# Mixture-of-experts stage of a transformer block in f32: another order of the gate, up and down products, and the low parts of the weights on one engine

## The chip, the cores and the metric

One core of one Trainium2 chip runs the whole block. The metric is device time in microseconds (us) of one launch; a profile of one execution shows each engine (PE = TensorE, with PEld its weight loads; ACT = ScalarE; DVE = VectorE; POOL = GpSimd; SP = SyncE, which here only issues DMAs).

## What is computed

The block is attention plus pooling plus convolution, an output projection, and then an expert-choice feed-forward network and a last normalisation. The change touches only the expert part:

```
aff = softmax(h @ w_router)                     # 1024 rows, 16 experts
g, idx = top_k(aff.T, 128)                      # each expert takes 128 rows
xg = h[idx]                                     # 16 x 128 x 2048
y = (silu(xg @ w_gate) * (xg @ w_up)) @ w_down * g
x = x + mod[5] * scatter_add(idx, y);  out = rmsnorm(x, final_g)
```

Per expert `w_gate` and `w_up` are 2048 x 1024 and `w_down` is 1024 x 2048, all f32: 24 MiB of weights an expert, read once from device memory, 384 MiB in all.

## The kernel before, in words

**Split products.** A product in f32 is made of three products in the fp32r format: high x high, high x low and low x high. A weight's high part is a cast on ACT (line 1393), its low part is the weight minus the high part (line 1397), on DVE, and for every third half unit on POOL. The activations are split in the same way after a transpose on PE (`transpose_split`, lines 1457 to 1465).

**Units.** The weights come in 24 units of 1 MiB an expert (`units`, from line 1349): a unit is two k-tiles of 128 rows by 1024 columns, so two half units. `fetch` (line 1371) loads a unit into one of 11 buffers (8 in the pool `er`, 3 in `er1`) through SP's queue; `half_unit` splits half a unit into one of 6 buffers `es_t`, asks for the load of the unit 11 places on, and hands the parts to 6 matmuls of 512 columns (3 products, 2 column halves), all through the helper at line 176. An expert thus has 48 half units and 288 such matmuls.

**Order within an expert** (from line 1504). The units of gate and up alternate, both results growing in two PSUM tiles `gu`. Then come Silu on ACT (line 1526), the product with up on DVE (line 1527), four groups of transposes for the next expert's rows (`turn_rows`: `xh`, `xl`, one buffer each) and the gather of the rows of the expert after that, two groups of transposes for this expert's hidden rows (`hh`, `hl`), and then down, as two halves of 8 half units, through one PSUM tile `dn`. DVE scales each half into `y` (line 1555), and a POOL-queue DMA adds `y` into the rows of `acc` (line 1559). A row of multipliers `M5` is built by `on_rows` ahead of the first expert: POOL makes diagonal tiles, PE multiplies them by ones.

**The last expert** also carries the eight final tiles (`final_tile`: load from `acc`, normalise, store), placed by the list `fin` at eighths of the gate-up part and quarters of the down halves; they use `er` buffers and SP's queue.

**Queues.** Every engine works its own queue in order. The order of a queue is not quite the written one: a list scheduler with a simulated timeline places the instructions, so next-expert matmuls can stand between those of the last down steps.

Of the kernel before, what the change touches and what calls it, by code (L numbers as in the profile page):

```python
# [9 lines left out]
F32 = mybir.dt.float32  # L10
F32R = mybir.dt.float32r
# [3 lines left out]
AF = mybir.ActivationFunctionType  # L15
ALU = mybir.AluOpType
# [4 lines left out]
P = 128  # L21
D = 2048
KT = D // P
# [5 lines left out]
NQB = SEQ // QB  # L29
HEADS = 8  # L30
NE = 16
CAP = 128
FF = 1024
NFT = FF // P
# [16 lines left out]
    first=58,  # L51
# [31 lines left out]
    er=8,  # L83
    e0=[3, 7, 11],
    eh=4,
    fin=[2, 4, 6, 8, 10, 11, 12, 13],
    wdve=0,
    z_val=3,
    z_n1=1,
# [41 lines left out]
def raw(ap):  # L131
    return ap.bitcast(F32)
# [36 lines left out]
def block_kernel(tc, I, out, dbg=None):  # L169
    nc = tc.nc  # L170
    pe, act, dve, gp, sp = nc.tensor, nc.scalar, nc.vector, nc.gpsimd, nc.sync
# [3 lines left out]
    def mm(o, l, r, start=True, stop=True):  # L175
        return pe.matmul(o, l, r, start=start, stop=stop, skip_group_check=True)  # L176
# [12 lines left out]
    acc = dr.tile([SEQ, D], F32, name="acc")  # L189
# [35 lines left out]
    fg_col = colB[:, 49:65]  # L225
# [1120 lines left out]
        ln2(i)  # L1346
    mk.close("lnx")
    er0 = mk("er0", bufs=3, side="right")
    units = []
    for e in range(NE):  # L1350
        for k in range(KT // 2):
            units.append((e, "g", k))
            units.append((e, "u", k))
        for half in range(2):
            for k in range(4):
                units.append((e, "d", (half, k)))

    def unit_src(u):
        e, kind, k = u
# [28 lines left out]
    def split(i, kk, early=None):  # L1388
        if i < len(units) and (i, kk) not in splits:
            fetch(i)  # L1390
            r = raws[i][:, kk]
            s = es_.tile([P, 2, 1024], F32R, name="es_t", tag="es")
            c = act.copy(s[:, 0], r)  # L1393
            if early:
                nosync(tc, c, last_exp[0])
            on_gp = 2 * i + kk < 4 if early else (2 * i + kk) % 3 == 2
            lo = (gp if on_gp else dve).tensor_tensor(s[:, 1], r, raw(s[:, 0]), op=ALU.subtract)  # L1397
            if early and not on_gp:
                nosync(tc, lo, early)
            splits[i, kk] = s  # L1400

    def half_unit(i, kk):
        split(i, kk)
        if kk == 0:
            fetch(i + PRE)
        else:
            raws.pop(i)
        return splits.pop((i, kk))
# [42 lines left out]
    def gather(e):  # L1451
        xg = ex.tile([P, D], F32, name="xg", tag="xg", bufs=1)
        ins = gp.indirect_dma_start(out=xg, out_offset=None, in_=h2S,
                                    in_offset=bass.IndirectOffsetOnAxis(ap=idxT[:, e:e + 1], axis=0))
        return xg, ins

    def transpose_split(x, n, hi, lo):
        for g in range(n // 4):
            t = pet.tile([P, 512], F32, name="tre", tag="tr")
            for q in range(4):  # L1460
                k = 4 * g + q
                pe.transpose(t[:, q * P:(q + 1) * P], x[:, k * P:(k + 1) * P], ident)  # L1462
            tv = t.rearrange("p (k n) -> p k n", n=P)
            act.copy(hi[:, 4 * g:4 * g + 4], tv)
            dve.tensor_tensor(lo[:, 4 * g:4 * g + 4], tv, raw(hi[:, 4 * g:4 * g + 4]), op=ALU.subtract)

    def final_rows(x, j):
        rms_stats(x, j, [ex.tile([P, D], BF16, name="dump_f", tag="xg", bufs=1)])
        dve.scalar_tensor_tensor(x, x, rst[:, j:j + 1], FG, op0=ALU.mult, op1=ALU.mult)

    def final_tile(i):
        xf = er.tile([P, D], F32, name="xf", tag="er")
        sp.dma_start(xf, acc[i * P:(i + 1) * P])
        final_rows(xf, i)
        sp.dma_start(out[i * P:(i + 1) * P], xf)

    ui = 0
    xg = [gather(0)]
    for i in range(PRE, PRE + 3):
        fetch(i, gp, xg[0][1])  # L1480

    def turn_rows(e):
        xh = ex.tile([P, KT, P], F32R, name="xh", tag="xh", bufs=1)
        xl = ex.tile([P, KT, P], F32R, name="xl", tag="xl", bufs=1)
        transpose_split(xg.pop()[0], KT, xh, xl)
        if 0 < e + 1 < NE:
            xg.append(gather(e + 1))
        return xh, xl

    xnext = turn_rows(0)  # L1490
    ones = ex.tile([P, P], F32, name="ones")
    dve.memset(ones, 1.0)

    def on_rows(dst, col):
        for g in range(4):
            t = pet.tile([P, 512], F32, name="tre", tag="tr")
            for q in range(4):
                dg = ex.tile([P, P], F32, name="dg", tag="dg", bufs=2)
                gp.tensor_scalar(dg, ident, col[:, 4 * g + q:4 * g + q + 1], 1.0, op0=ALU.mult, op1=ALU.mult)  # L1499
                mm(t[:, q * P:(q + 1) * P], ones, dg)  # L1500
            act.copy(dst[:, g * 512:(g + 1) * 512], t)

    M5 = ex.tile([P, D], F32, name="M5")
    on_rows(M5, mods[:, 5])
    for e in range(NE):
        xh, xl = xnext
        gu = [pgu.tile([P, 1024], F32, name=f"gu{i}", tag=f"gu{i}") for i in range(2)]
        for k2 in range(KT // 2):
            if e == NE - 1:
                if k2 == 0:  # L1510
                    FG = er.tile([P, D], F32, name="FG", tag="er")
                    on_rows(FG, fg_col)
                for i in range(NQB * 2):
                    if T["fin"][i] == k2:
                        final_tile(i)
            for w in range(2):
                for kk in range(2):
                    k = 2 * k2 + kk
                    s = half_unit(ui, kk)
                    for lhs, wl, first, last in ((xh, 0, True, False), (xh, 1, False, False), (xl, 0, False, True)):  # L1520
                        for c in range(2):
                            mm(gu[w][:, c * 512:(c + 1) * 512], lhs[:, k, :], s[:, wl, c * 512:(c + 1) * 512],
                               start=(k == 0 and first), stop=(k == KT - 1 and last))
                ui += 1
        hs = ex.tile([P, FF], F32, name="hs", tag="hs", bufs=1)
        act.activation(hs, gu[0], AF.Silu)
        dve.tensor_tensor(hs, hs, gu[1], op=ALU.mult)
        if e + 1 < NE:
            xnext = turn_rows(e + 1)
        hh = ex.tile([P, NFT, P], F32R, name="hh", tag="hh", bufs=1)  # L1530
        hl = ex.tile([P, NFT, P], F32R, name="hl", tag="hl", bufs=1)
        transpose_split(hs, NFT, hh, hl)
        y = ex.tile([P, D], F32, name="y", tag="y", bufs=1)
        last = e == NE - 1
        if last:
            xr = er.tile([P, D], F32, name="xr", tag="er")
            gp.indirect_dma_start(out=xr, out_offset=None, in_=acc,
                                  in_offset=bass.IndirectOffsetOnAxis(ap=idxT[:, e:e + 1], axis=0))
        for half in range(2):
            dn = pdn.tile([P, 1024], F32, name="dn", tag="dn")  # L1540
            for k2 in range(4):
                if last:
                    for i in range(NQB * 2):
                        if T["fin"][i] == 8 + 4 * half + k2:
                            final_tile(i)
                for kk in range(2):
                    k = 2 * k2 + kk
                    s = half_unit(ui, kk)
                    for lhs, wl, first, fin in ((hh, 0, True, False), (hh, 1, False, False), (hl, 0, False, True)):
                        for c in range(2):  # L1550
                            mm(dn[:, c * 512:(c + 1) * 512], lhs[:, k, :], s[:, wl, c * 512:(c + 1) * 512],
                               start=(k == 0 and first), stop=(k == NFT - 1 and fin))
                ui += 1
            hsl = slice(half * 1024, (half + 1) * 1024)
            dve.scalar_tensor_tensor(y[:, hsl], dn, gT[:, e:e + 1], M5[:, hsl], op0=ALU.mult, op1=ALU.mult)  # L1555
            if last:
                dve.tensor_tensor(y[:, hsl], y[:, hsl], xr[:, hsl], op=ALU.add)
        if not last:
            gp.indirect_dma_start(out=acc, out_offset=bass.IndirectOffsetOnAxis(ap=idxT[:, e:e + 1], axis=0),
                                  in_=y, in_offset=None, compute_op=ALU.add)  # L1560
        else:
            final_rows(y, 8)
            gp.indirect_dma_start(out=out, out_offset=bass.IndirectOffsetOnAxis(ap=idxT[:, e:e + 1], axis=0),
                                  in_=y, in_offset=None)

    if "h2" in dbg:
        sp.dma_start(dbg["h2"], h2S)
# [30 lines left out]
```

## Time and profile before

| | before |
|---|---|
| median of 3 runs | 3542.62 us (3541.07 to 3546.62) |
| the profiled execution, own time | 3547.89 us |
| its span | 3546.1 us |
| mean granted TensorE clock | 0.937 |
| first and last matmul of the expert stage | 2185.2 and 3516.8 us |
| busy over the span | PE 88%, DVE 70%, ACT 52%, POOL 47% |

The span is read by stretches: the expert stage is its last 1361 us, and an expert's period is the time from the second half of one down product to that of the next. "Idle before" in a row is the time in which the engine stood still ahead of those instructions, with what ended it. "DMA share" is the mean busy share of the 16 DMA engines in a stretch; records of packets overlap a little, so it can read just over 1. A clock of 1.00 is the upper of TensorE's two levels, 0.50 the lower.

### The profile page before, as it was taken

What the parts mean: (1) busy time and instruction counts of PE and PEld (TensorE: products, weight loads), DVE (VectorE), ACT (ScalarE), POOL (GpSimd) and SP (SyncE); (2) the same over time, 40 slices, a digit from 0 to 9 for tenths busy, and PEclk for the clock granted to TensorE, in tenths of its full rate; (3) what the DMA queues carried; (4) which work ended last, traced back from release to release, by engine and by line L of the source; (5) the groups of instructions that cost most, each with busy time, mean ns of one, the idle gap of its engine ahead of it and who ended that gap; (6) DMA issues with size and microseconds to landing.
All of it is one profiled execution on the core that took longest, in us unless ns stands there. A gap on an engine that the chain in (4) does not pass through costs nothing.

```text
span 3546.1 us, 48685 instructions
## 1 busy us (share of the span) xinstructions
PE 3130.5 (88%) x18527; PEld 2672.3 (75%) x18527; DVE 2496.6 (70%) x2523; ACT 1833.1 (52%) x2585; POOL 1673.7 (47%) x863
## 2 busy tenths in 40 slices
PE   7789999999897979788999795988889989999985
PEld 4678889888786868668899794777667767777774
DVE  5676766641356566765756687888888888888877
ACT  5433322451355545544554344666666666666665
POOL 1551100110554544535666776655555555665664
PEclk9899999999998989889999997999999999999997
DMA  9667787632654544555878777999999898999987
GB/s 309 185 210 244 276 282 263 198 107 79 198 168 129 159 146 142 178 171 180 278 232 279 246 257 265 320 326 341 330 331 329 315 333 325 333 334 326 343 303 283
DMA packets 489564, 891.23 MB, mean 251 GB/s; under 512 B 24913, under 2 KB 339874, under 8 KB 478450
## 3 DMA queue, kind: packets, MB, share of 16 engines
q1 hardware_dynamic: 465488, 791.42, 64.8%
q0 software_dynamic: 23744, 96.68, 9.1%
q8 instruction: 145, 2.38, 0.3%
q14 instruction: 89, 0.73, 0.1%
q10 hardware_dynamic: 98, 0.03, 0.0%
HBM read 797.80 MB, written 90.23 MB: 250 GB/s over the span
## 4 chain that ended last, share of the span: by engine, by line
PE 28%; DVE 12%; issue 10%; POOL 6%; DMA 3%; ACT 3%; POOLq 0%; SPq 0%; DVEq 0%; ACTq 0%
PE gu L176 10%; PE dn L176 8%; DVE es_t L1397 6%; PE gm L176 5%; POOL w_split L424 3%; PE sc L176 1%; POOL es_t L1397 1%; PE tre L1462 1%; PE av L176 1%; ACT es_t L1393 1%; DMA cv_z<-zS 1%; DMA w_raw<-in_w_out 1%; DVE nm L935 1%; DMA nbc<-sclS 1%; POOL dg L1499 1%
## 5 line engine op out<-in xcount | busy, mean ns | idle before, releaser
L1397 DVE TENSOR_TENSOR es_t<-er_t,es_t 128x1024 fp32r<-128x1024 f32 x509 | 1008.3, 2026 | 166.3 <-ACT es_t L1393 165.5
L1393 ACT CAST es_t<-er_t 128x1024 fp32r<-128x1024 f32 x768 | 797.2, 1050 | 343.1 <-PE gu L176 173.2
L1397 POOL TENSOR_TENSOR es_t<-er_t,es_t 128x1024 fp32r<-128x1024 f32 x259 | 719.8, 2781 | 456.4 <-ACT es_t L1393 456.2
L424 POOL TENSOR_TENSOR w_split<-w_raw,w_split 128x1024 fp32r<-128x1024 f32 x208 | 549.3, 2649 | 388.0 <-ACT w_split L423 367.1
L176 PE MATMUL g_x<-hxh,w_split 128*128 128x512 f32 (+3 forms) x2560 | 596.9, 344 | 18.7 <-DVE w_split L424 13.0
L176 PE MATMUL gu<-es_t,xh 128*128 128x512 f32 x2048 | 579.6, 400 | 11.9 <-DVE es_t L1397 10.9
L423 ACT CAST w_split<-w_raw 128x1024 fp32r<-128x1024 f32 x288 | 301.7, 1049 | 373.9 <-PE g_x L176 109.0
L176 PEld LDWEIGHTS gu<-es_t,xh 128*128 128x128 f32 x2048 | 378.8, 188 | 112.0 <-DVE es_t L1397 25.3
L176 PEld LDWEIGHTS g_x<-hxh,w_split 128*128 128x128 f32 x2560 | 402.6, 192 | 66.0 <-DVE w_split L424 14.6
L176 PE MATMUL gm<-w_split,mxh 128*128 128x256 f32 x2048 | 392.7, 290 | 9.1 <-POOL w_split L424 3.5
L176 PEld LDWEIGHTS gm<-w_split,mxh 128*128 128x128 f32 x2048 | 327.3, 195 | 16.6 <-DVE oy L1097 4.8
L176 PE MATMUL g_x<-hxl,w_split 128*128 128x256 f32 (+1 forms) x1280 | 337.1, 341 | 1.3 <-DVE hxl L396 1.3
L176 PE MATMUL dn<-es_t,hh 128*128 128x512 f32 x1024 | 307.7, 422 | 28.2 <-DVE y L1555 26.6
L176 PE MATMUL gu<-es_t,xl 128*128 128x512 f32 x1024 | 322.7, 396 | 0.0
L176 PE MATMUL gm<-w_split,mxl 128*128 128x256 f32 x1024 | 296.5, 290 | 1.1 <-DMA mxl<-mixP 1.1
L935 DVE TENSOR_REDUCE nm<-sc 128x1 f32<-128x1280 f32 x128 | 190.6, 1489 | 130.7 <-PE sc L176 85.5
L176 PE MATMUL gm<-hbh,w_split 128*128 128x256 f32 x1280 | 255.2, 294 | 21.3 <-ACT e_raw L497 14.6
L176 PEld LDWEIGHTS dn<-es_t,hh 128*128 128x128 f32 x1024 | 204.1, 203 | 86.0 <-ACT es_t L1393 29.8
L308 DVE SCALAR_TENSOR_TENSOR ada_a<-ada_w,st,ada_a 128x1024 f32<-128x1024 f32 x150 | 226.6, 1510 | 42.0 <-DMA ada_w<-in_w_ada 38.9
L176 PEld LDWEIGHTS gm<-hbh,w_split 128*128 128x128 f32 x1280 | 209.1, 197 | 28.8 <-ACT e_raw L497 18.2
L176 PEld LDWEIGHTS gu<-es_t,xl 128*128 128x128 f32 x1024 | 192.0, 188 | 45.8
L176 PEld LDWEIGHTS g_x<-hxl,w_split 128*128 128x128 f32 x1280 | 201.5, 191 | 24.9 <-DVE hxl L396 2.5
(300 smaller groups left out, 4887.5 us busy)
## 6 DMA issues: line engine op xcount, KB each, us to landing
er_t<-in_w_down SPq DMA_DIRECT2D x128, 1024.0 KB, 7.9
er_t<-in_w_gate SPq DMA_DIRECT2D x127, 1024.0 KB, 9.5
er_t<-in_w_up SPq DMA_DIRECT2D x126, 1024.0 KB, 6.6
ada_w<-in_w_ada SPq DMA_DIRECT2D x192, 512.0 KB, 5.5
w_raw<-in_w_in SPq DMA_DIRECT2D x160, 512.0 KB, 4.5
w_raw<-in_w_out SPq DMA_DIRECT2D x128, 512.0 KB, 5.0
ks<-kS POOLq DMA_DIRECT2D x16, 1280.0 KB, 8.3
vh<-vS POOLq DMA_DIRECT2D x16, 640.0 KB, 5.8
```

The source lines that it names most:

```text
L176: return pe.matmul(o, l, r, start=start, stop=stop, skip_group_check=True)
L308: dve.scalar_tensor_tensor(a, wt, col(k), a, op0=ALU.mult, op1=ALU.add)
L423: act.copy(s[:, 0], r)
L424: lo_eng.tensor_tensor(s[:, 1], r, raw(s[:, 0]), op=ALU.subtract)
L935: r = dve.tensor_reduce(nm, s, axis=AX, op=ALU.max, negate=True)
L1393: c = act.copy(s[:, 0], r)
L1397: lo = (gp if on_gp else dve).tensor_tensor(s[:, 1], r, raw(s[:, 0]), op=ALU.subtract)
L1462: pe.transpose(t[:, q * P:(q + 1) * P], x[:, k * P:(k + 1) * P], ident)
L1499: gp.tensor_scalar(dg, ident, col[:, 4 * g + q:4 * g + q + 1], 1.0, op0=ALU.mult, op1=ALU.mult)
```

## The change

- A list `plan` of stages takes the place of the loop body. The order is gate 0, up 0, then for experts 1 to 14: gate e, first half of down e-1, up e, second half of down e-1. At the end come both halves of down 14, then gate 15, up 15 and both halves of down 15. The units are fetched in that order; gate and up no longer alternate.
- Work beside the products is hung on steps (`beside`): the transposes of the rows of expert e (2 to 14) on steps 1, 3, 5, 7 of the second half of down e-2; those of the hidden rows of e (0 to 13) on steps 2 and 4 of gate e+1; `M5` on steps 6 to 12 of gate 1 instead of ahead of expert 0. Expert 1's rows are turned at the end of up 0, expert 14's hidden rows at the end of down 13, and expert 15's rows and hidden rows at the ends of down 14 and up 15.
- The down halves of experts 14 and 15 use `dn` and then a gate or up PSUM tile in turn.
- The final tiles are placed anew, over gate, up and down of expert 15.
- All low parts of weights, but for the four at the very start, are taken on DVE.

```diff
-    fin=[2, 4, 6, 8, 10, 11, 12, 13],
+    fin=[("g", 6), ("g", 12), ("u", 2), ("u", 8), ("u", 13), ("0", 2), ("0", 6), ("1", 2)],
...
+    plan = [("g", 0), ("u", 0)]
+    for e in range(1, NE - 1):
+        plan += [("g", e), ("d", e - 1, 0), ("u", e), ("d", e - 1, 1)]
+    plan += [("d", NE - 2, 0), ("d", NE - 2, 1), ("g", NE - 1), ("u", NE - 1), ("d", NE - 1, 0), ("d", NE - 1, 1)]
     units = []
-    for e in range(NE):
-        for k in range(KT // 2):
-            units.append((e, "g", k))
-            units.append((e, "u", k))
...
+    for kind, e, *half in plan:
+        units += [(e, kind, (half[0], k) if half else k) for k in range(4 if half else KT // 2)]
...
-            on_gp = 2 * i + kk < 4 if early else (2 * i + kk) % 3 == 2
+            on_gp = early and 2 * i + kk < 4
...
+    def turn_x(e, g):
+        if g == 0:
+            X_[e] = [ex.tile([P, KT, P], F32R, name=n, tag=n, bufs=1) for n in ("xh", "xl")]
+        turn_group(xg[e][0], g, *X_[e])
+        if g == 3:
+            xg.pop(e)
+            if e + 1 < NE:
+                xg[e + 1] = gather(e + 1)
...
+    for e in range(1, NE):
+        stage = ("u", 0) if e == 1 else ("d", e - 2, 1) if e < NE - 1 else ("d", NE - 2, 1)
+        for g in range(4):
+            add(stage, 15 if e == 1 else 2 * g + 1, turn_x, e, g)
     for e in range(NE):
...
+        for g in range(2):
+            if e < NE - 2:
+                add(("g", e + 1), 2 + 2 * g, turn_h, e, g)
+            elif e == NE - 2:
+                add(("d", e - 1, 1), 7, turn_h, e, g)
+            else:
+                add(("u", e), 15, turn_h, e, g)
+    for g in range(4):
+        add(("g", 1), 6 + 2 * g, on_rows, M5, mods[:, 5], [g])
+    for i, (kind, k) in enumerate(T["fin"]):
+        add((kind, NE - 1) if kind in "gu" else ("d", NE - 1, int(kind)), k, final_tile, i)
...
+    for stage in plan:
+        kind, e = stage[:2]
...
+        if kind == "d":
+            half = stage[2]
+            bank = pdn if half == 0 or e < NE - 2 else pgu
+            o = bank.tile([P, 1024], F32, name="dn", tag="dn" if bank is pdn else "gu" if e == NE - 2 else "gg")
...
+            o, lhss, nk = pgu.tile([P, 1024], F32, name="g" + kind, tag="g" + kind), X_[e], KT
+        for k in range(nk):
+            s = half_unit(ui, k % 2)
+            for lhs, wl, first, fin in ((lhss[0], 0, True, False), (lhss[0], 1, False, False), (lhss[1], 0, False, True)):
+                for c in range(2):
+                    mm(o[:, c * 512:(c + 1) * 512], lhs[:, k, :], s[:, wl, c * 512:(c + 1) * 512],
+                       start=(k == 0 and first), stop=(k == nk - 1 and fin))
...
+            for f, args in beside.get((stage, k), ()):
+                f(*args)
```

`turn_group` is one group of `transpose_split` as it was: four transposes, the cast on ACT, the subtraction on DVE.

## Rows read from the trace of the kernel before

**Rows 1.** The page, DMA busy tenths and GB/s in 40 equal slices:
```profile
DMA  9667787632654544555878777999999898999987
GB/s 309 185 210 244 276 282 263 198 107 79 198 168 129 159 146 142 178 171 180 278 232 279 246 257 265 320 326 341 330 331 329 315 333 325 333 334 326 343 303 283
```

**Rows 2.** Stretches of the expert stage: us, each engine's busy, PEclk, DMA share, GB/s:
```profile
2185.00:2261.29 76.29, 68.86 (x314) 55.28 (x313) 57.09 (x39) 50.86 (x56) 56.00 (x31) 0.94 0.84 299
2261.29:3334.13 1072.84, 967.88 (x4048) 761.64 (x4049) 925.14 (x534) 701.50 (x715) 616.68 (x235) 0.94 0.92 331
3334.13:3415.00 80.87, 74.36 (x313) 58.97 (x314) 68.07 (x40) 52.39 (x54) 45.09 (x18) 0.94 0.88 317
3415.00:3491.50 76.50, 64.62 (x285) 50.99 (x283) 62.84 (x38) 50.24 (x52) 60.21 (x31) 0.93 0.80 278
3491.50:3546.10 54.60, 23.36 (x92) 18.19 (x92) 34.00 (x25) 24.32 (x24) 17.67 (x13) 0.75 0.76 300
```

**Rows 3.** Timeline of one gap between up and down (2733 to 2744 us):
```profile
2733.91 0.63 PE L176 MATMUL gu<-es_t,xl 128*128 128x512 f32 x2
...
2739.17 1.94 PE L1462 MATMUL tre<-cst,xg 128*128 128x128 f32 x8 [4.63 <-DVE xl L1465]
...
2743.45 2.07 PE L176 MATMUL dn<-es_t,hh 128*128 128x512 f32 x4
```

**Rows 4.** Stretches of 3 us across a gap (columns as in rows 2):
```profile
2652.00:2655.00 3.00, 0.00 (x0) 0.00 (x0) 2.98 (x3) 2.04 (x4) 1.61 (x1) 0.99 1.02 359
2655.00:2658.00 3.00, 2.02 (x9) 1.65 (x10) 2.71 (x4) 1.17 (x2) 0.35 (x1) 0.50 0.87 314
```

**Rows 5.** Waits, thirteen periods from 2261 to 3334 us: us, times, longest:
```profile
PE dn L176 <- DVE y L1555: 21.6, 13, 1.9
```

**Rows 6.** The DMA queue's own waits over the same thirteen periods:
```profile
SPq L1371 <- DVE es_t L1397: 749.2, 313, 9.9
```

**Rows 7.** Short stretches (columns as in rows 2), two dips, then three full ones:
```profile
2664.00:2670.00 6.00, 6.00 (x27) 4.86 (x26) 4.30 (x3) 4.60 (x5) 4.21 (x2) 1.00 0.49 164
2748.00:2754.00 6.00, 6.00 (x27) 4.83 (x26) 3.44 (x3) 4.40 (x5) 3.79 (x2) 1.00 0.35 135
...
2619.00:2649.00 30.00, 28.63 (x121) 22.35 (x121) 29.48 (x14) 19.95 (x20) 18.34 (x7) 1.00 1.00 384
2703.00:2739.00 36.00, 30.21 (x128) 23.31 (x126) 35.09 (x18) 24.59 (x25) 21.25 (x8) 0.97 1.01 379
...
2622.00:2625.00 3.00, 3.00 (x15) 2.41 (x14) 2.48 (x3) 2.88 (x3) 1.75 (x1) 1.00 1.03 421
```

**Rows 8.** The chain that ended last: 39 matmuls in a row:
```profile
2273.19 9.12 PE gu L176 x39
```

**Rows 9.** DMA of the thirteen periods: bytes, two kinds of queue, median us to landing:
```profile
DMA packets 88661, 355.16 MB, mean 331 GB/s; under 512 B 5408, under 2 KB 5408, under 8 KB 85275
...
q0 software_dynamic: 3744, 27.26, 9.8%
...
acc<-y,idxT POOLq DMA_INDIRECT x13, 12.0
xg<-h2S,idxT POOLq DMA_INDIRECT x13, 9.1
```

**Rows 10.** Groups by line, thirteen periods: count, busy us, mean ns, idle before:
```profile
L1397 DVE TENSOR_TENSOR es_t<-er_t,es_t 128x1024 fp32r<-128x1024 f32 x417 | 833.8, 2047 | 127.5 <-ACT es_t L1393 126.9
L1397 POOL TENSOR_TENSOR es_t<-er_t,es_t 128x1024 fp32r<-128x1024 f32 x209 | 580.4, 2778 | 401.3 <-ACT es_t L1393 401.2
L1462 PE MATMUL tre<-cst,xg 128*128 128x128 f32 x200 | 41.6, 340 | 58.6 <-DVE xl L1465 58.6
```

**Rows 11.** Timeline of DVE, two low parts: beside a POOL subtraction, then alone:
```profile
2757.94 2.21 DVE L1397 TENSOR_TENSOR es_t<-er_t,es_t 128x1024 fp32r<-128x1024 f32 x1
2760.91 1.23 DVE L1397 TENSOR_TENSOR es_t<-er_t,es_t 128x1024 fp32r<-128x1024 f32 x1 [0.77 <-ACT es_t L1393]
```

**Rows 12.** Timeline of PE: transposes between gate and up matmuls of a running expert:
```profile
2690.17 0.49 PE L1462 MATMUL tre<-cst,xg 128*128 128x128 f32 x3
```

**Rows 13.** Timeline of the end: the last matmuls and the last store:
```profile
3516.54 0.62 PE L176 MATMUL dn<-es_t,hl 128*128 128x512 f32 x2
...
3538.24 1.03 POOL L1563 DMA_INDIRECT out<-y,idxT  x1 [4.16 <-DMA out<-xf]
```

More of the change, by code (lines that the diff above doesn't have):

```diff
@@ L1348, in block_kernel @@
     er0 = mk("er0", bufs=3, side="right")
+    plan = [("g", 0), ("u", 0)]
+    for e in range(1, NE - 1):
+        plan += [("g", e), ("d", e - 1, 0), ("u", e), ("d", e - 1, 1)]
+    plan += [("d", NE - 2, 0), ("d", NE - 2, 1), ("g", NE - 1), ("u", NE - 1), ("d", NE - 1, 0), ("d", NE - 1, 1)]
     units = []
-    for e in range(NE):
-        for k in range(KT // 2):
-            units.append((e, "g", k))
-            units.append((e, "u", k))
-        for half in range(2):
-            for k in range(4):
-                units.append((e, "d", (half, k)))
+    for kind, e, *half in plan:
+        units += [(e, kind, (half[0], k) if half else k) for k in range(4 if half else KT // 2)]
     def unit_src(u):
@@ L1455, in gather, with turn_group @@
         return xg, ins
[L1457 to L1465, printed above, removed]
+    def turn_group(x, g, hi, lo):
+        t = pet.tile([P, 512], F32, name="tre", tag="tr")
+        for q in range(4):
+            k = 4 * g + q
+            pe.transpose(t[:, q * P:(q + 1) * P], x[:, k * P:(k + 1) * P], ident)
+        tv = t.rearrange("p (k n) -> p k n", n=P)
+        act.copy(hi[:, 4 * g:4 * g + 4], tv)
+        dve.tensor_tensor(lo[:, 4 * g:4 * g + 4], tv, raw(hi[:, 4 * g:4 * g + 4]), op=ALU.subtract)
     def final_rows(x, j):
@@ L1475, in final_tile, with on_rows @@
         sp.dma_start(out[i * P:(i + 1) * P], xf)
-    ui = 0
-    xg = [gather(0)]
+    xg = {0: gather(0)}
     for i in range(PRE, PRE + 3):
         fetch(i, gp, xg[0][1])
[L1482 to L1490, printed above, removed]
     ones = ex.tile([P, P], F32, name="ones")
     dve.memset(ones, 1.0)
-    def on_rows(dst, col):
-        for g in range(4):
+    M5 = ex.tile([P, D], F32, name="M5")
+    def on_rows(dst, col, groups=range(4)):
+        for g in groups:
             t = pet.tile([P, 512], F32, name="tre", tag="tr")
@@ L1501, in on_rows @@
             act.copy(dst[:, g * 512:(g + 1) * 512], t)
-    M5 = ex.tile([P, D], F32, name="M5")
-    on_rows(M5, mods[:, 5])
-    for e in range(NE):
[L1506 to L1533, printed above, removed]
-        last = e == NE - 1
[L1535 to L1541, printed above, removed]
-                if last:
[L1543 to L1560, printed above, removed]
-        else:
-            final_rows(y, 8)
-            gp.indirect_dma_start(out=out, out_offset=bass.IndirectOffsetOnAxis(ap=idxT[:, e:e + 1], axis=0),
-                                  in_=y, in_offset=None)
@@ new lines, in block_kernel, with turn_h @@
+    X_, H_, hs_, y_ = {}, {}, {}, {}
+    def turn_x(e, g):
[6 more added lines that the diff above has]
+                xg[e + 1] = gather(e + 1)
+    def turn_h(e, g):
+        if g == 0:
+            H_[e] = [ex.tile([P, NFT, P], F32R, name=n, tag=n, bufs=1) for n in ("hh", "hl")]
+        turn_group(hs_[e], g, *H_[e])
@@ new lines, in block_kernel, with add @@
+    beside = {}
+    def add(stage, step, f, *args):
+        beside.setdefault((stage, step), []).append((f, args))
+    for e in range(1, NE):
+        stage = ("u", 0) if e == 1 else ("d", e - 2, 1) if e < NE - 1 else ("d", NE - 2, 1)
+        for g in range(4):
+            add(stage, 15 if e == 1 else 2 * g + 1, turn_x, e, g)
+    for e in range(NE):
+        for g in range(2):
[5 more added lines that the diff above has]
+                add(("u", e), 15, turn_h, e, g)
@@ new lines, in block_kernel, with add_rows @@
+    for g in range(4):
+        add(("g", 1), 6 + 2 * g, on_rows, M5, mods[:, 5], [g])
+    for i, (kind, k) in enumerate(T["fin"]):
+        add((kind, NE - 1) if kind in "gu" else ("d", NE - 1, int(kind)), k, final_tile, i)
+    def add_rows(e):
+        if e < NE - 1:
+            gp.indirect_dma_start(out=acc, out_offset=bass.IndirectOffsetOnAxis(ap=idxT[:, e:e + 1], axis=0),
+                                  in_=y_.pop(e), in_offset=None, compute_op=ALU.add)
+        else:
+            final_rows(y_[e], 8)
+            gp.indirect_dma_start(out=out, out_offset=bass.IndirectOffsetOnAxis(ap=idxT[:, e:e + 1], axis=0),
+                                  in_=y_.pop(e), in_offset=None)
@@ new lines, in block_kernel @@
+    for g in range(4):
+        turn_x(0, g)
+    ui, xr = 0, None
+    for stage in plan:
+        kind, e = stage[:2]
+        last = e == NE - 1
+        if kind == "d":
+            half = stage[2]
+            bank = pdn if half == 0 or e < NE - 2 else pgu
+            o = bank.tile([P, 1024], F32, name="dn", tag="dn" if bank is pdn else "gu" if e == NE - 2 else "gg")
+            lhss, nk = H_[e], NFT
+            if half == 0:
+                y_[e] = ex.tile([P, D], F32, name="y", tag="y", bufs=1)
+                if last:
+                    xr = er.tile([P, D], F32, name="xr", tag="er")
+                    gp.indirect_dma_start(out=xr, out_offset=None, in_=acc,
+                                          in_offset=bass.IndirectOffsetOnAxis(ap=idxT[:, e:e + 1], axis=0))
+        else:
+            if stage == ("g", NE - 1):
+                FG = er.tile([P, D], F32, name="FG", tag="er")
+                on_rows(FG, fg_col)
+            o, lhss, nk = pgu.tile([P, 1024], F32, name="g" + kind, tag="g" + kind), X_[e], KT
[5 more added lines that the diff above has]
+                       start=(k == 0 and first), stop=(k == nk - 1 and fin))
+            ui += k % 2
+            if k == nk - 1:
+                if kind == "g":
+                    hs_[e] = ex.tile([P, FF], F32, name="hs", tag="hs", bufs=1)
+                    act.activation(hs_[e], o, AF.Silu)
+                elif kind == "u":
+                    dve.tensor_tensor(hs_[e], hs_[e], o, op=ALU.mult)
+                else:
+                    y, hsl = y_[e], slice(half * 1024, (half + 1) * 1024)
+                    dve.scalar_tensor_tensor(y[:, hsl], o, gT[:, e:e + 1], M5[:, hsl], op0=ALU.mult, op1=ALU.mult)
+                    if last:
+                        dve.tensor_tensor(y[:, hsl], y[:, hsl], xr[:, hsl], op=ALU.add)
+                    if half == 1:
+                        add_rows(e)
+            for f, args in beside.get((stage, k), ()):
+                f(*args)
```

## The prediction
> **What bounds the kernel now.** I read the page's slices first: from about 2185 us on the DMA engines are over 80% busy at 315 to 343 GB/s until the last slices [rows 1], so the expert stage could be held by the loads, by PE, or by neither all the time. The stretches answer that [rows 2]: thirteen whole experts take 1072.84 us, 82.5 us each, with PE busy 90% and DMA 92%. Neither is full. The timeline of one gap between up and down says why [rows 3]: the last up matmuls end at 2733.91 + 0.63 = 2734.54, PE then stands for 4.63 us until VectorE has taken a low part of the next rows, runs transposes, at a clock of 0.50 if it is as in the gap before [rows 4], and reaches the first down matmul only at 2743.45. So some 9 us an expert pass with only 16 transposes in them, and the short wait for the down bank between the two halves is 21.6 / 13 = 1.7 us more [rows 5]. In the gap no half unit is consumed, so the 11 load buffers fill; SP's queue then waits for a low part to free one, 313 times, 9.9 us at the longest [rows 6], and the DMA share falls a little later to 0.49 and 0.35 [rows 7]. The DMA engines lose their 8% there. In long stretches outside the gap the share is 1.00 and 1.01 [rows 7]: there the loads are already at their limit while PE eats the stock. The bound now is thus a PE gap that also stops the loads.
>
> **What each resource needs for one expert.** PE: 39 matmuls took 9.12 us [rows 8], 0.234 us each; 288 x 0.234 = 67.4 us. Eight transposes took 1.94 us at the low clock [rows 3], so 24 are 5.8 us there and half, 2.9 us, at the high one: 70.3 us. DMA: 0.92 x 82.5 = 75.9 us at a full share. The bytes are 355.16 / 13 = 27.3 MB [rows 9]. VectorE now: its busy 925.14 us [rows 2] less 833.8 us of low parts [rows 10] leaves 91.3 / 13 = 7.0 us for all else. ACT: 701.5 / 13 = 54 us [rows 2]. So with the gap gone the loads are what is left, 76 us, with PE 6 us and the others further below.
>
> **The change, part by part.**
>
> *Low parts on VectorE.* 209 / 13 = 16 subtractions an expert leave GpSimd [rows 10]. One low part takes VectorE 1.23 us alone and 2.21 us beside GpSimd's [rows 11]; the mean now is 2.05 us [rows 10]. After it, 48 x 1.23 = 59.0 us plus 7.0 us = 66 us, against 32 x 2.05 + 7 = 73 us now. VectorE thus does more and is busy less, and the 2.78 us latency of a GpSimd low part goes too. Bounds for one low part: 1.23 us and the mean of 2.05 us; I take 1.23, since nothing but DMA issue is left on GpSimd in this stage. On the path this costs nothing as long as the loads need 76 us.
>
> *Gate of the next expert between up and down.* Silu, the product, the two hidden groups and their splits now have the 16 half units of a gate beside them, 16 x 6 x 0.234 = 22 us. The gap [rows 3] goes for experts 1 to 13, thirteen of sixteen. It stays in part at expert 0 (the rows of expert 1 are turned behind up 0) and at expert 14 (its hidden rows are turned between two downs that share one `hh`), and whole at expert 15. The two down halves lie an up apart, so the 1.7 us bank wait goes as well. What is late next is the load: PE would be through in 70.3 us and the weights come in 76.
>
> *Row transposes on steps 1, 3, 5, 7 of the second down half.* The one `xh` is free there, as up has ended. Each group puts one cast in ACT's queue and one subtraction in VectorE's, with the weight splits of later steps behind them, and PE waits for those if they come late. Below, nothing: transposes that already stand between gate and up matmuls show no idle time ahead of them [rows 12]. Above, the 4.63 us wait [rows 3] shared by two groups, 2.3 us each. I take under 1 us, nearer to the lower end, because six split buffers run ahead; up to 6 x 1 us is hidden in PE's slack of 6 us.
>
> *Gathers and the adding DMA.* The queue of GpSimd loses its subtractions, so both issue no later than now. The next gather has nearly an expert until its rows are turned and lands in 9.1 us; the adding DMA takes 12.0 us [rows 9] and `y` is not written again until a gate, 22 us, and a down half have passed. Both cost nothing on the path. Their own share stays: the queue they use takes 9.8% [rows 9].
>
> *`M5` into gate 1.* 16 diagonals and products leave expert 0 and stand in gate 1, ahead of the first use at down 0. Nothing there waits; plus or minus 3 us, taken as 0.
>
> *Order of the loads.* The same 24 units, on the same queue, with gate and up apart instead of in turn: no row shows either order at another rate, so 0, with the spread of the full stretches (379 to 384 GB/s [rows 7]) as its bounds, 1% of the stage, about 10 us either way.
>
> *The end.* The final tiles start at step 6 instead of 8 of expert 15's 48, and end at 42 as now; their 8 loads and 8 stores stand on SP's queue ahead of weight loads, and a store waits there for its normalisation. The tail from the last matmul to the last store's issue, 3516.54 to 3538.24 [rows 13], keeps its chain. Bounds: 8 us won (the last store waits 4.16 us for other stores now) to 12 us lost; taken as 0. The buffers at the end of expert 14 will be emptier than now, as no gap has filled them; this is in the sum as DMA idle time that stays.
>
> **The sum.** DMA idle time in the stage is (1 - share) x length [rows 2]: 12.2 us in expert 0, 85.8 in the thirteen experts, 9.7 and 15.3 in the next two stretches and 13.1 at the end. With PE faster than the loads there is always a free buffer, so the idle time of the thirteen should go to between 0 (the full stretches) and 85.8; I take 1.5% of 987 us, 15 us, nearest to the full stretches. That is 71 us won. Of the 9.7 us (around expert 14, whose gap is then partly hidden) 8 go, of the 15.3 us 5, of the rest nothing: 84 us. The remaining gaps cost nothing, since 11 empty buffers keep loading through them. The profiled execution took 3547.89 us, so 3464 for it; the median is 5.3 us below that execution: **3459 us**, a period of (1072.84 - 71) / 13 = 77.1 us.
>
> **Rivals.**
>
> *The loads can go faster and PE becomes the bound.* For it: single stretches of 3 us reach 421 GB/s [rows 7]; 27.3 MB at that rate would be 65 us, below PE's 70.3. Against it: the 30 and 36 us stretches stay at 384 and 379 GB/s with a full share, without the adding DMA in them. Then 13 x (82.5 - 71) = 150 us plus about 10 at the ends: 3383 us. The HBM Reference of the Trainium skill (Specifications) states that a core streaming alone gets about 425 GB/s and one whose neighbour streams too about 358 GB/s; an estimate by its two figures is 64 and 76 us an expert. The trace sits between, 379 to 384 over the long stretches, and decides for neither.
>
> *Partial.* Groups of about 1.5 us a piece, or a clock that falls again and again, eat PE's slack: after 3 us without matmuls PE ran at 0.50, the lower of its two levels (1.2 of 2.4 GHz) [rows 4], and waits for loads may do the same in small. At 79.5 us an expert: 13 x 3 + 6 = 45 us won, 3498 us.
>
> *No gain.* The scheduler puts the queues nearly back to the old order, or a share of 0.92 is the most the loads hold on average, the dips being their own: 3540 us. The 36 us at 1.01 speak against the second, the dips right behind gaps too.
>
> *Slower: the turn groups become a convoy.* Six groups an expert now stand inside the stream of products, each with ACT's cast and VectorE's subtraction ahead of later weight splits in queues worked in order. If each stops PE for that upper bound of 2.3 us [rows 3], PE needs 70.3 + 6 x 2.3 = 84.1 us, over today's 82.5: 13 x 1.6 = 21 us lost, 3564 us. It decides from (82.5 - 70.3) / 6 = 2.0 us a group. Against it stand the transposes without a wait [rows 12].
>
> **How the numbers follow.** Forecast 0.66 (its own range 3438 to 3485: a steady idle share of 0 to 4% and the end's bounds), PE bound 0.09, partial 0.13, no gain 0.06, convoy 0.06. Two runs differ by up to 0.16% here, so 0.2%, 7 us, is what a measurement can tell. Faster is the sum of the first three, 0.88; same 0.06; slower 0.06. The range 3425 to 3515 holds the forecast and the partial case and leaves out most of the rest.
>
> **What would show it.** Right: a period near 77 us in the thirteen experts, DMA share 0.97 or more there, low parts on VectorE at 1.2 to 1.3 us, no idle time of PE of over 3 us between up and down, ACT's casts waiting for loads of `er_t` instead of for PE, and hardly any wait of SP's queue for low parts. Wrong: SP's queue still waiting for free buffers with a share near 0.92 (the gap has moved, not gone), low parts near 2 us with GpSimd at rest, a share of 0.98 at 82 us (the loads slower in the new order), or PE idle ahead of each of the six groups.

## The result and the profile after

The changed kernel takes **3407.5 us** (median of 4 runs, 3404.39 to 3411.36), against 3541.85 us for the kernel before in the same comparison: a ratio of 0.9628, 95% interval 0.9613 to 0.9642. The sign was forecast, the size was not: 134 us instead of 84, below the range of 3425 to 3515 us and 24 us above the rival in which PE is the bound.

The stretches of the changed kernel come first (columns as in [rows 2]): one early expert, one late expert and twelve whole periods.

```profile
2312.25:2382.20 69.95, 69.95 (x314) 56.58 (x313) 63.98 (x58) 54.15 (x56) 2.76 (x2) 1.00 1.02 383
...
2526.64:2601.60 74.96, 72.28 (x314) 57.51 (x313) 62.24 (x58) 51.92 (x57) 3.77 (x2) 0.98 0.97 365
...
2312.25:3197.64 885.39, 859.86 (x3757) 686.09 (x3756) 747.76 (x684) 625.29 (x662) 46.52 (x25) 0.98 0.98 369
```

A period is now 885.39 / 12 = 73.8 us instead of 82.5. These twelve periods alone give 12 x 8.7 = 104 of the 136.5 us by which the span fell (3546.1 to 3409.6). The tail keeps its length: from the last matmul to the end of the span 29 us before [rows 13], 28 us now. Two things are to be seen. In the early expert PE is busy for all of its 69.95 us, at a clock of 1.00 and beside a DMA share of 1.02. In the late one, which stands for seven of the twelve, PE stands still for 2.7 us, runs a little under full clock, and the period is 74.96 us.

What the groups, the waits and SP's queue say of the same twelve periods answers [rows 10], [rows 3] and [rows 6]:

```profile
L1397 DVE TENSOR_TENSOR es_t<-er_t,es_t 128x1024 fp32r<-128x1024 f32 x574 | 665.8, 1220 | 64.5 <-ACT es_t L1393 63.5
...
ACT hs L1572 <- PE gg L176: 55.4, 12, 5.4
DVE hs L1574 <- PE gu L176: 46.5, 11, 4.7
ACT xh L1463 <- PE gu L176: 44.9, 11, 4.1
DVE y L1577 <- PE dn L176: 26.6, 11, 2.6
...
PE gu L176 <- DVE es_t L1397: 20.4, 10, 2.0
...
SPq L1371 <- DVE es_t L1397: 756.4, 287, 8.0
```

A low part takes VectorE 1.220 us, as forecast, and VectorE is busy 747.76 / 12 = 62 us a period. The loads are not what is left: SP's queue still waits for a free buffer 287 times, and in the whole list of waits no engine waits for a weight load. What is left is a chain in two queues. Silu, up's product, the casts of the next rows and the scaling of `y` each wait for PE at the head of ACT's or VectorE's queue, with weight splits behind them that could run (e7_behind and e8_behind_x below tell which of these waits count). The timeline of one period shows what that leads to:

```profile
2617.44 1.05 ACT L1393 CAST es_t<-er_t 128x1024 fp32r<-128x1024 f32 x1 [0.35 <-PE gg L176]
2623.91 1.03 ACT L1572 ACTIVATE hs<-gg 128x1024 f32<-128x1024 f32 x1 [5.42 <-PE gg L176]
...
2635.42 1.29 DVE L1577 SCALAR_TENSOR_TENSOR y<-dn,gT,M 128x1024 f32<-128x1024 f32 x1 [2.62 <-PE dn L176]
2636.62 16.17 DVE L1397 TENSOR_TENSOR es_t<-er_t,es_t 128x1024 fp32r<-128x1024 f32 x14
...
2637.90 0.73 PE L176 MATMUL gu<-es_t,xh 128*128 128x512 f32 x2 [2.05 <-DVE es_t L1397]
```

ACT makes its last cast at 2617.44, waits 5.42 us for the end of gate, and the stock of split half units shrinks. Then VectorE waits 2.62 us for the end of down, and PE runs dry for 2.05 us in front of up.

### The profile page after: what moved, and what is told of

Read it like the earlier page. It is cut to its first block, busy times and chain, and to the rows that moved or that the text cites. A ratio compares the mean times of both kernels' runs of the same rounds, so it can differ in the third digit from the quotient of the medians.

```text
span 3409.6 us, 48373 instructions
## 1 busy us (share of the span) xinstructions
PE 3091.2 (91%) x18527; PEld 2653.7 (78%) x18527; DVE 2376.6 (70%) x2778; ACT 1807.7 (53%) x2585; POOL 975.4 (29%) x608
## 5 line engine op out<-in xcount | busy, mean ns | idle before, releaser
L1397 DVE TENSOR_TENSOR es_t<-er_t,es_t 128x1024 fp32r<-128x1024 f32 x764 | 893.1, 1224 | 100.2 <-ACT es_t L1393 97.6
L1393 ACT CAST es_t<-er_t 128x1024 fp32r<-128x1024 f32 x768 | 776.7, 1052 | 182.3 <-PE gu L176 102.0
L176 PE MATMUL gu<-es_t,xh 128*128 128x512 f32 x1024 | 293.9, 408 | 21.1 <-DVE es_t L1397 21.1
L176 PE MATMUL dn<-es_t,hh 128*128 128x512 f32 x1024 | 300.4, 405 | 9.4 <-DVE es_t L1397 5.2
L176 PE MATMUL gg<-es_t,xh 128*128 128x512 f32 x1024 | 290.4, 400 | 1.1 <-ACT xh L1463 1.1
L1453 POOL DMA_INDIRECT xg<-h2S,idxT x16 | 22.0, 1375 | 823.9 <-PE tre L1461 674.6
L176 PEld LDWEIGHTS gu<-es_t,xh 128*128 128x128 f32 x1024 | 197.5, 194 | 73.6 <-DVE es_t L1397 26.4
L176 PEld LDWEIGHTS dn<-es_t,hh 128*128 128x128 f32 x1024 | 190.4, 190 | 61.2 <-DVE es_t L1397 13.9
L176 PEld LDWEIGHTS gg<-es_t,xh 128*128 128x128 f32 x1024 | 190.8, 189 | 47.2 <-DVE es_t L1397 1.9
```

## The experiments

**Each edit alone.** The first two runs take the change apart.

```diff
 e1_order_only, on the changed kernel
-            on_gp = early and 2 * i + kk < 4
+            on_gp = 2 * i + kk < 4 if early else (2 * i + kk) % 3 == 2
 e2_low_only, on the kernel before
-            on_gp = 2 * i + kk < 4 if early else (2 * i + kk) % 3 == 2
+            on_gp = early and 2 * i + kk < 4
```

> The changed kernel, but every third low part goes to GpSimd as before: the new order alone. Theory A (the new order with its longer runs of loads from one tensor carries the gain): about 100 of the 134 us stay, some 3440 us; low parts on VectorE at about 2.0 us, 73 us of VectorE an expert, just under the period. Theory B (the low parts on VectorE alone carry half or more): 3480 us or more.

> The kernel before, with all low parts on VectorE: that edit alone. Theory A: the gap between up and down only gets shorter by the waiting low part, 1 to 2 us an expert, so 3510 to 3525 us. Theory B: 3480 us or less.

The new order alone: 3549.01 us, a ratio to the kernel before of 1.0028 (1.0015 to 1.0041). It is slower, not 100 us faster. The low parts alone: 3486.68 us, 0.9856 (0.9839 to 0.9874), 53 us faster and near the 3480 of theory B. Alone they give -9 and +53 us, together 134: the order is worth something only with the other edit, and the two are worth more than their sum. Theory A falls. Theory B is nearer, but the low parts alone carry 40% of the gain and not half. Seven periods of the order alone and ten of the low parts alone, as stretches:

```profile
2547.77:3143.91 596.14, 521.20 (x2184) 399.60 (x2184) 507.66 (x289) 366.60 (x386) 346.91 (x126) 0.98 0.91 321
```

```profile
2346.97:3138.05 791.08, 732.09 (x3114) 584.01 (x3113) 654.09 (x572) 544.42 (x551) 33.01 (x20) 0.96 0.93 345
```

With the order alone a period is 596.14 / 7 = 85.2 us and PE still stands for 75 / 7 = 10.7 us of it; with the low parts alone it is 79.1 us and 5.9 us. The groups and the waits of the order alone (2400 to 3120 us) show the reason:

```profile
L1397 DVE TENSOR_TENSOR es_t<-er_t,es_t 128x1024 fp32r<-128x1024 f32 x276 | 567.3, 2107 | 79.5 <-ACT es_t L1393 78.6
...
L1397 POOL TENSOR_TENSOR es_t<-er_t,es_t 128x1024 fp32r<-128x1024 f32 x137 | 393.0, 2878 | 279.7 <-ACT es_t L1393 279.6
...
PE gg L176 <- DVE es_t L1397: 35.6, 34, 1.9
...
PE gu L176 <- DVE es_t L1397: 20.5, 8, 2.6
...
PE dn L176 <- DVE es_t L1397: 19.9, 24, 1.4
```

While GpSimd works, VectorE makes two low parts in 2 x 2.11 = 4.2 us for every three half units, 1.40 us a half unit, and that is what PE takes to use one (6 x 0.234). With 7 us of other work an expert VectorE is no faster than PE. So no stock can build up beside running products, and PE waits for low parts in gate, up and down alike. By this reading the old gap was the time in which VectorE caught up, and without it the same time appears as many short waits; no run shows that part by itself, but e9_behind_gp below tests whether the rate alone still holds the order back. At 1.22 us alone VectorE gains on PE with every half unit. The Trainium skill (SBUF — State Buffer, SBUF: two separate sides) states that a VectorE operation with two SBUF inputs and a GpSimd one that reads SBUF block each other whole; 1.22 against 2.11 us here agrees that the two slow each other, but a mean does not show a lock.

**The order of the loads.** In the kernel before gate and up loads alternate; after the change 8 loads in a row come from one tensor. Single windows of 3 us with a full share moved 352 to 367 GB/s before (2727 to 2736 us) and 408 to 414 after (2646.6 to 2655.6 us), so the alternation was a suspect.

```diff
 e3_src_in_turn, on the kernel before
-        return I["w_gate" if kind == "g" else "w_up"][0, e, k * 256:(k + 1) * 256, :]
+        n = 2 * k + (kind == "u")
+        return I["w_gate" if n < 8 else "w_up"][0, e, n % 8 * 256:(n % 8 + 1) * 256, :]
 e6_alt_src, on the changed kernel
-        return I["w_gate" if kind == "g" else "w_up"]...
+        return I["w_gate" if (kind == "g") == (k % 2 == 0) else "w_up"]...
```

> The kernel before, with the 16 gate and up loads of an expert taken from eight gate units and then eight up units, instead of in turn; the products then use the wrong ones of the two. Theory L (loads that alternate between two tensors are slower): the DMA engines' time for the weight loads of an expert falls from 67.7 us to about 64.3 us, as in the changed kernel, and the total by little (0 to 20 us), as PE's gap stays. Theory G (the loads became faster because GpSimd rests, or because of the order of the products): 67.7 us stays.

> The changed kernel, with gate units and up units swapped at every second load, so that consecutive loads alternate between the two tensors; the products then use the wrong ones. Theory L: the weight loads take 67.7 us of the DMA engines an expert again, and with the adding DMA the period is 76 us or more: 3425 to 3450 us. Theory G: 64.3 us and 3408 us as in the changed kernel.

Neither source order matters: 3538.86 us, 0.9995 (0.9983 to 1.0008), and 3409.26 us, 0.9635 (0.9617 to 0.9653). The weight queue's share and bytes from 2400 to 3120 us, for the kernel before and the first run, then for the changed kernel and the second run, give 0.807 x 720 / 216.80 = 2.68 us of the 16 engines per MB for the first run and 2.58 for the second, against 2.69 and 2.58 in the kernels they come from. Theory L falls.

```profile
q1 hardware_dynamic: 56470, 217.70, 81.2%
...
q1 hardware_dynamic: 56229, 216.80, 80.7%
```

```profile
q1 hardware_dynamic: 63660, 245.42, 87.8%
...
q1 hardware_dynamic: 63575, 245.07, 87.8%
```

**Loads or queues.** Two runs relieve PE and the loads in turn; there is one execution of each.

```diff
 e4_no_third, on the changed kernel
-            ... ((lhss[0], 0, True, False), (lhss[0], 1, False, False), (lhss[1], 0, False, True)):
+            ... ((lhss[0], 0, True, False), (lhss[0], 1, False, True)):
 e5_half_loads, on the changed kernel
+            n = 512 if 14 <= i < 360 else 1024
-            ... eng.dma_start(r, unit_src(units[i])...
+            ... eng.dma_start(r[:, :, 0:n], unit_src(units[i])...[:, :, 0:n]
...
```

> The changed kernel without the third product (low x high), so PE needs 192 x 0.234 + 3 = 48 us an expert. Theory D (the loads are what is left at 75 us): the period stays at 73 to 76 us. Theory Q (instructions placed too early in ACT's and VectorE's queues make PE run dry): the period falls to the next limit, the loads' own service time of about 72 us; if it falls well below 70 us the loads were never near their limit.

> The changed kernel with half the bytes of each weight load from unit 14 to unit 359 (the left half of the columns is used twice). Theory D: the period falls to PE's 70 us. Theory Q: it stays at 73 to 75 us, with the same idle times of PE in front of up.

Without the third product the period is 68.85 us (688.53 us for ten, below) and the run 3316.36 us. Casts now wait for loads (97 us from 2400 to 3120 us, most of it for gate's), so the loads are near their own limit: 27.3 MB at 396 to 397 GB/s. They need at most 69 us an expert and not the 76 of the prediction. SP's queue waits for buffers here too (the last row, 2400 to 3120 us), so that wait alone does not tell whether the loads are the limit; the casts do.

```profile
2422.11:3110.64 688.53, 584.50 (x2161) 371.54 (x2160) 620.14 (x572) 510.23 (x551) 71.99 (x20) 0.96 1.03 396
...
ACT es_t L1393 <- DMA er_t<-in_w_gate: 69.3, 39, 5.6
...
SPq L1371 <- DVE es_t L1397: 471.1, 186, 9.7
```

With half the bytes the period is 69.8 us with PE busy throughout, 3360.08 us. That would speak for theory D, but it decides nothing, as the queues changed too (their order is the list scheduler's, and this edit also changes how the splits read a load). Silu now stands where it need not wait, 0.34 us instead of 5.42:

```profile
2457.18:3155.57 698.39, 698.39 (x3121) 564.21 (x3121) 639.26 (x571) 539.15 (x550) 70.31 (x20) 1.00 0.68 211
...
2619.66 1.03 ACT L1578 ACTIVATE hs<-gg 128x1024 f32<-128x1024 f32 x1 [0.34 <-PE gg L176]
```

**The places in the queues, by themselves.** The loads stay whole; only the emission of three instructions moves.

```diff
 e7_behind, on the changed kernel
+            parts[i, kk] = (c, lo)
...
+                def finish(behind=None, ...):   # Silu, up's product or y, as before
...
+                    if behind:
+                        nosync(tc, ins, behind[j])
...
+                    held.append(finish)
+            if k == 5 and held:
+                held.pop()(parts[ui - k % 2, k % 2])
 e8_behind_x, on e7_behind
-            add(stage, 15 if e == 1 else 2 * g + 1, turn_x, e, g)
+            add(stage, 15 if e == 1 else (5, 6, 7, 7)[g], turn_x, e, g)
 e10_silu_only, on e7_behind
-                if (kind == "u" and e in (0, NE - 1)) or stage in (("d", NE - 3, 1), ("d", NE - 1, 1)):
+                if kind != "g":
```

> The changed kernel with Silu, the product with up and the scaling of y emitted six half units later and held behind the weight split of that step in their queue, so that they no longer stand ahead of splits that could run. Theory Q: PE's idle time in front of up and down goes, the period falls from 75 to 71 to 72.5 us in most experts, 3370 to 3390 us. Theory D: within 5 us of the changed kernel.

> As the run before, and the transposes of the next rows moved from steps 1, 3, 5, 7 of the second down half to steps 5, 6, 7, 7. Theory Q: ACT's wait of 4 us for the end of up in front of the first of these casts goes too, 3365 to 3390 us. Theory D: no gain; the four groups crowded at the end could cost 1 to 3 us an expert.

> The changed kernel with only Silu held behind a later split in ACT's queue. If the 5.4 us wait of ACT for the end of gate is what lets the splits run dry: period 70 to 72 us, 3360 to 3375 us. If the waits of VectorE for up's product and for y count as well: 3380 to 3400 us.

Held behind later splits, the three instructions no longer stop their queues: **3359.18 us**, 0.9485 (0.9469 to 0.9501), the fastest version here, 48 us under the changed kernel and below the 3370 us that was expected at best. The loads' bytes and order are the same, so theory Q holds. Seven periods in a row:

```profile
2662.02:3154.36 492.34, 492.28 (x2186) 395.38 (x2185) 443.19 (x401) 369.25 (x386) 134.42 (x14) 1.00 1.02 389
```

PE stands still for 0.06 us in 492.34 us, and a period is 70.3 us: PE is the bound although every load is whole, with the loads' 69 us just beneath. The place of the row transposes changes nothing more (3359.19 us, 0.9484, 0.9468 to 0.9499). Silu alone is worth little: 3401.73 us, 0.9612 (0.9591 to 0.9634), an interval that overlaps the changed kernel's, and just over the 3380 to 3400 us expected if VectorE's waits count as well. Its waits from 2400 to 3100 us say why; the ends of down and up still stop VectorE, for longer now (55.4 / 10 = 5.5 us a wait at `y` instead of 26.6 / 11 = 2.4), and PE's wait in front of up stays:

```profile
DVE y L1579 <- PE dn L176: 55.4, 10, 5.9
...
DVE hs L1576 <- PE gu L176: 38.6, 9, 4.7
...
PE gu L176 <- DVE es_t L1397: 18.4, 9, 2.0
```

**Is GpSimd's share a matter of queue places too?** The same held instructions, with every third low part on GpSimd (the edit of e1_order_only on e7_behind; behind a GpSimd low part VectorE's last one is taken).

> The new order with Silu, up's product and the scaling of y held behind later splits (as in the run that reached 3359 us), but every third low part on GpSimd. Theory S (with GpSimd at work the splits come no faster than PE uses them: two low parts on VectorE at 2.1 us in the time of three half units at 1.40 us, and VectorE has 7 us of other work an expert): the period is 75 to 82 us, 3420 to 3520 us in all. Theory Q (only the early places in the queues made the new order useless without the other edit): 70 to 73 us, below 3400 us.

3470.61 us, 0.981 (0.979 to 0.9829), a period of (3252.19 - 2397.87) / 11 = 77.7 us from the scalings of `y`. Theory S holds: good places are worth 78 us over the order alone, and GpSimd's part still costs 111 us against e7_behind. VectorE is busy 93% of the time, at 2.09 us a low part, so with good places its own rate is what is left:

```profile
2400.00:3100.00 700.00, 657.03 (x2814) 514.78 (x2813) 651.13 (x373) 478.58 (x496) 428.97 (x163) 0.98 0.98 352
...
L1397 DVE TENSOR_TENSOR es_t<-er_t,es_t 128x1024 fp32r<-128x1024 f32 x290 | 591.0, 2090 | 41.4 <-ACT es_t L1393 41.0
```

The DMA share is 0.98 at 352 GB/s, while it is 1.03 at 397 without the third product. So a share near 1 is not a limit, and the last two runs look for what makes the difference.

**How many loads are in flight.** One execution of each.

```diff
 e11_few_buffers, on e4_no_third
-    er=8,
+    er=4,
 e12_look4, on e4_no_third
-    PRE = T["er"] + 3
+    PRE = 4
```

> The run without the third product (loads at 397 GB/s, 68.9 us an expert, landing 19 to 22 us after issue), with 4 instead of 8 load buffers beside the other 3, so at most 7 instead of 11 loads in flight. Theory F (the rate of the loads depends on how many are in flight, and the share reads near 1 long before): the rate falls well below 397 GB/s, the period to 72 us or more, with a DMA share still of 0.95 or more. Rival (the rate depends on GpSimd's rest or VectorE's work, not on the number): 68 to 70 us, 395 GB/s.

> The run without the third product (396 to 397 GB/s with up to 11 or 7 load buffers), with each load asked for 4 units ahead instead of 11, so that only about 2 to 3 loads are in flight while the buffers drain, as in the kernel before. GpSimd rests as in the changed kernel. Theory F (few loads in flight make each byte take longer while the DMA share still reads near 1): 350 GB/s or less at a share of 0.92 or more, 2.65 us of the 16 engines per MB instead of 2.50. Rival (the time per byte comes from what GpSimd and VectorE do): the time per MB stays at 2.50 us, and a lower rate shows as a lower share.

With 7 buffers nothing changes in the loads' rate (396 GB/s), against what theory F expected of this run. The run takes 3355.76 us, 39 us more, with the last scaling of `y` 44 us later; the last expert's final tiles take from the same buffers, which may be the reason. With 4 units of lookahead the run takes 3427.21 us. From 2400 to 3100 us the weight queue and the loads' times to landing, first without either limit, then, below a stretch's row, with 4 units:

```profile
q1 hardware_dynamic: 66444, 256.16, 91.6%
...
er_t<-in_w_gate SPq DMA_DIRECT2D x84, 1024.0 KB, 21.5
er_t<-in_w_down SPq DMA_DIRECT2D x80, 1024.0 KB, 18.8
er_t<-in_w_up SPq DMA_DIRECT2D x80, 1024.0 KB, 18.6
```

```profile
2400.00:3100.00 700.00, 575.43 (x2040) 367.70 (x2038) 591.77 (x537) 483.08 (x519) 31.64 (x18) 0.92 1.00 367
...
q1 hardware_dynamic: 61718, 237.93, 89.8%
...
er_t<-in_w_up SPq DMA_DIRECT2D x80, 1024.0 KB, 7.3
er_t<-in_w_down SPq DMA_DIRECT2D x75, 1024.0 KB, 7.7
er_t<-in_w_gate SPq DMA_DIRECT2D x72, 1024.0 KB, 10.8
```

The time per MB rises from 0.916 x 700 / 256.16 = 2.50 to 0.898 x 700 / 237.93 = 2.64 us, almost the 2.68 of the kernel before (0.814 x 700 / 212.31), at a share of 1.00 and with GpSimd at rest. Loads land in 7 to 11 us here and in 5 to 8 in the kernel before, against 19 to 22 us where many are in flight. The rate fell to 367 GB/s, not to the 350 that theory F gave, but the time per byte moved as it said. An estimate from the same views (loads times their median time to landing, over 700 us) gives 1.9, 2.8, 3.3, 3.8, 4.8 and 6.9 loads in flight in the kernel before, e12_look4, the changed kernel, e7_behind, e11_few_buffers and e4_no_third, at 2.68, 2.64, 2.57, 2.54, 2.50 and 2.50 us per MB. So the number in flight moves the time per byte, and by these runs from about five loads on it gives nothing more, which fits the rate that 7 buffers kept. GpSimd's work may have a small part in it beside that: e9_behind_gp, with 2.5 in flight, has 0.874 x 700 / 227.20 = 2.69 us per MB. That stays open.

## Why the prediction was right in sign and wrong in size

- **The gap in PE as the place of the loss:** right. Its time can be had: 82.5 to 73.8 us in the changed kernel, to 70.3 with the queues in order.
- **One expert's needs.** PE 70.3 us: right to a tenth (e7_behind). VectorE 66 us at 1.23 us a low part: 62 us, at a mean of 1.220 for one and 16.17 / 14 = 1.16 us in a row. The loads, "0.92 x 82.5 = 75.9 us at a full share": **this step failed.** It took the share for a service time. The share reads 1.00 at 367 GB/s and 1.03 at 397, so it is no measure of the rate. The full stretches [rows 7], too, had few loads in flight: from 2619 to 2649 us SP's queue waited for buffers for 27.9 of 30 us, and ten loads that land in 7.5 us make 2.5 at a time, by estimate. Even so the rate of those stretches, 379 to 384 GB/s, makes 71 to 72 us of 27.3 MB, so the prediction's own rows spoke against 75.9. With a product taken from PE the loads took 69 us, and in e7_behind whole loads kept up with a period of 70.3. Every number behind the step, the 15 us of idle time kept and the period of 77.1 us, leaned on it; what held the changed kernel at 73.8 us was the waits in ACT's and VectorE's queues.
- **Low parts on VectorE, "on the path this costs nothing":** wrong. Alone it is worth 53 us, and without it the new order is worth less than nothing. The sum of VectorE's work, 73 us of 82.5, looked like cover. What counted was the rate beside running products: 2.05 x 2 / 3 = 1.37 us a half unit plus 7.0 / 48 = 0.15 us of other work against PE's 1.40, which could have been worked out from the same rows [rows 8, 10].
- **The gate between up and down:** the loss goes only if splits can be stocked while products run. The sum gave the order all 84 us; it is worth -9 us alone and 134 - 53 = 81 us once VectorE is quick.
- **Row transposes under 1 us a group:** they cost PE nothing in e7_behind, and moving them changed nothing. But of the instructions that wait at a queue's head the prediction looked only at these; Silu, up's product and `y` were costed by the work that hides them, not by what stands behind them. The places of these three cost the 48 us between the changed kernel and e7_behind.
- **The rivals.** "PE becomes the bound" had the nearest time (3383 us) and the right mechanism for e7_behind; it was given 0.09 on the grounds of the two long stretches. The Trainium skill's HBM Reference (Specifications) has 425 GB/s for a core that streams alone; 397 GB/s, the adding DMA's bytes included, is nearer to that than to its 358. The convoy of the six groups did not come: PE has no idle time ahead of the row transposes in the changed kernel or in e1_order_only. What makes e1_order_only slower than the kernel before is another queue of waits, for low parts at 2.11 us behind instructions placed too early; in the changed kernel 2.7 us of idle time a period are left of it.

## What to carry to other kernels

Before a stall is costed as won, work out whether the engines that feed it can keep up without the pause: here the supply per half unit only equalled the demand, and the new order won nothing until it was faster. A DMA share near 1 is not by itself a limit: look whether any engine waits for a load, and take work from the consumer to find the real one. In a queue worked in order, an instruction that waits for another engine is better placed behind later work that can run without it, as long as nothing needs its result sooner.

## What had not been expected of the hardware

The 16 DMA engines show a share of 1.00 at 367 GB/s and of 1.03 at 397, with the same 1 MiB loads; the number of loads in flight is what differed. And in e7_behind, whose VectorE is busy 90% of the time, the issue of the adding DMA on GpSimd's queue grew from a median of 2.4 to 18.2 us (`y` as a tile, kernel before, then e7_behind):

```profile
L1559 POOL DMA_INDIRECT acc<-y,idxT x15: 2383/2401/2438, 2277.1 to 3433.1; - x15
```

```profile
L1534 POOL DMA_INDIRECT acc<-y,idxT x15: 1560/18217/21622, 2308.2 to 3254.3; - x15
```

It costs that kernel next to nothing, since `y` is not written again for two stages: VectorE waits for that DMA three times, 6.2 us in all, and PE stands for 0.06 us in the seven periods above. Its cause was not tried.
